# Sums of weight blocks on GpSimd, in two alternating buffers, in a two-layer hybrid decoder trunk

## The chip, the cores and the metric

The kernel runs on one core of one Trainium2 chip. The metric is the device time of one execution in microseconds (us). The time before is the median of three runs, 1335.95 us (1334.69 to 1336.82). Below, PE is the matrix engine (TensorE), PEld its weight loads, DVE VectorE, ACT ScalarE, POOL GpSimd, and SP the engine that issues the weight transfers.

## The reference, cut to what matters

Two layers over 528 positions (512 inputs behind 16 learned ones) of width 1024. Each layer is a token mixer and a gated feed-forward block with a causal convolution, each followed by a layer norm. The change touches the arithmetic of the projections only, so these lines matter:

```python
def short_conv_mixer(h, w_in, conv_w, w_out):
    b_gate, c_gate, xv = jnp.split(h @ w_in, 3, axis=-1)
    u = causal_dwconv(c_gate * xv, conv_w)
    return (b_gate * u) @ w_out

def conv_ffn(h, w_up, conv_w, w_down):
    u, gate = jnp.split(h @ w_up, 2, axis=-1)
    u = causal_dwconv(u, conv_w)
    return (jax.nn.silu(u) * gate) @ w_down
...
for i in range(DEPTH):
    ...   # mixer 0: chunked gated DeltaNet, mixer 1: short_conv_mixer
    h = layer_norm(ALPHA * h + mix, ln_mix_g[i], ln_mix_b[i])
    h = layer_norm(ALPHA * h + conv_ffn(h, ffn_w_up[i], ffn_conv[i], ffn_w_down[i]),
                   ln_ffn_g[i], ln_ffn_b[i])
```

## The kernel before

Activations lie channels down the partitions, positions along the row: `h` is 128 x 8 x 528 (8 blocks of 128 channels). Every float32 value that PE multiplies is split by `split` (L88, L89): ACT writes a rounded high part (`hh`, `gh`, `sumh`, and `wh` for weights), DVE the rest (`hl`, `gl`, `suml`, `wl`). A product is then three matmuls for each block of 128 rows, high by high, high by low, low by high (L272 to L274).

The order of stages is: the DeltaNet mixer (the first 370 us), its output projection, the first feed-forward block, the short convolution, the second feed-forward block. A feed-forward block works on its 22 channel strips in groups of 4, 6, 6 and 6 (`GROUPS`): an up stage makes the strips of `u` and `gate`, then `down` multiplies the group by its part of the down projection, eight output strips `pd` whose results DVE adds to `h` (L762 for the first group, L764 for later ones). The short convolution has groups of 2 and 6.

The first group of each block is computed plainly (`up`). The later groups go by **pairs** (`pairs`, L888): two weight strips and two halves of the positions form a 2 by 2 block product, which is computed with seven half-size products in place of eight, so the weights and the activations have to be added up in blocks first. A pair loads two raw strips, a and b. Its seven weight operands (`PREP`) are the blocks A11 and A12 (of a), A22 (of b) and four sums made by `sums`: S1 = both halves of b; S2 = S1 + A11; S3 = a half of b plus A11, written in place into b; S4 = S2 + A12. Before the change, DVE makes all four, and S1, S2 and S4 are one buffer `s`, overwritten in turn. There are 43 pairs in seven sections: three sections of 6 in each feed-forward block and one of 7 in the short convolution. On PE a pair takes its products in the order A11, S1, A22 of the pair before, S2, A12, S4 of the pair before, S3. A11, S2, S3 and A22 accumulate into one bank `px`, S1 and S4 into `pz`, and A12 goes to `pq`. Between the products ACT reads the running sum of `px` (L921 after A11, L927 after S2, L935 after S3, L940 after A22), and the next product into `px` cannot start before. DVE finishes with L932, L937, L944 and the gating (L846, L990). Six banks hold all of this.

The split weights live in a ring of 56 blocks (`room`): two tiles `wh0`/`wl0` and `wh1`/`wl1`. `pump` loads raw strips and splits them as far ahead as the ring and the raw buffers (four) allow. A scheduler fixes the order of each engine's instructions when the program is built, by its own timing model. On the chip each engine then takes its instructions strictly in that order, each waiting for its inputs.

The pools: `cpool` keeps constants for the whole run. `gp` holds the DeltaNet stage's buffers, and is given back when that stage ends; the later pools, `wpool2` with `s` among them, take that space.

Of the kernel before, what the change touches and what calls it, by code (L numbers as in the profile page):

```python
# [8 lines left out]
F32 = mybir.dt.float32  # L9
F32R = mybir.dt.float32r  # L10
F16 = mybir.dt.float16
U8 = mybir.dt.uint8
AF = mybir.ActivationFunctionType
ALU = mybir.AluOpType
PSUM = bass.MemoryType.PSUM

P = 128
# [13 lines left out]
CH = 106  # L31
# [3 lines left out]
LEVELS = (1, 2, 4, 8, 16, 32, 64)  # L35
# [18 lines left out]
NCST = 3 * P  # L54
# [19 lines left out]
def tile_hybrid_trunk(ctx, tc, xt, par, cst, msk, w_ba, w_qkv, w_z, w_ao, w_bi, w_bo, w_up, w_dn, out):  # L74
    nc = tc.nc
    V, S, G, TE = nc.vector, nc.scalar, nc.gpsimd, nc.tensor

    cpool = ctx.enter_context(tc.tile_pool(name="cpool", bufs=1))
    hpool = ctx.enter_context(tc.tile_pool(name="hpool", bufs=1))
    wpool = ctx.enter_context(tc.tile_pool(name="wpool", bufs=1))  # L80
    lnp = ctx.enter_context(tc.tile_pool(name="lnp", bufs=1))

    h = hpool.tile([P, KD, T], F32, name="h")
    hh = hpool.tile([P, KD, T], F32R, name="hh")
# [7 lines left out]


    par_sb = cpool.tile([P, NPAR], F32, name="par_sb")
    cst_sb = cpool.tile([P, NCST], F32, name="cst_sb")
    msk_sb = cpool.tile([P, len(LEVELS), CH], U8, name="msk_sb")
    ba_raw = lnp.tile([P, KD, 16], F32, name="ba_raw", tag="c", bufs=CB)
    ba_hi = lnp.tile([P, KD, 16], F32R, name="ba_hi", tag="c", bufs=CB)
    ba_lo = lnp.tile([P, KD, 16], F32R, name="ba_lo", tag="c", bufs=CB)
# [60 lines left out]
    pools = []  # L160
# [43 lines left out]
    def sums(job, what):  # L204

        a, b = job.raws
        a11, a12, a21, a22 = a[:, 0:4, :], a[:, 4:8, :], b[:, 0:4, :], b[:, 4:8, :]
        if what == "S1":
            job.s = pools[-1].tile([P, 4, P], F32, name=f"s{job.n}", tag="s", bufs=1)
            V.tensor_tensor(job.s, a21, a22, ALU.add)  # L210
        elif what == "S2":
            V.tensor_tensor(job.s, job.s, a11, ALU.add)
        elif what == "S3":
            V.tensor_tensor(a21, a21, a11, ALU.add)
        elif what == "S4":
            V.tensor_tensor(job.s, job.s, a12, ALU.add)
        own = {"A11": a11, "A12": a12, "A22": a22, "S3": a21}
        return own[what] if what in own else job.s

    def prep_step(job):  # L220

        pair = len(job.srcs) == 2
        what = PREP[len(job.units)] if pair else "all"
        u = room(4 if pair else job.nk)
        if u is None:
            return False
        job.units[what] = u
        if pair:
            split(u.hi, u.lo, sums(job, what))
        else:  # L230
            step = job.nk if job.n else 4
            for k in range(0, job.nk, step):
                split(u.hi[:, k : k + step, :], u.lo[:, k : k + step, :], job.raws[0][:, k : k + step, :])
        job.ready = len(job.units) == (len(PREP) if pair else 1)
        return True
# [50 lines left out]
    pump(2)  # L286

    ident = cst_sb[:, C_ID : C_ID + P]
    ident16 = cpool.tile([P, P], F16, name="ident16")
    V.tensor_copy(ident16, ident)  # L290
    tri = cst_sb[:CH, C_TRI : C_TRI + CH]
    strict = cst_sb[:CH, C_STR : C_STR + CH]
    strict_r = cpool.tile([P, CH], F32R, name="strict_r")
    V.tensor_copy(strict_r[:CH], strict)
    one1 = cpool.tile([P, P], F32, name="one1")
    V.memset(one1, 1.0)
    epsc = cpool.tile([P, 1], F32, name="epsc")
    V.memset(epsc, LN_EPS)
# [11 lines left out]
        return ap.unsqueeze(1).to_broadcast([ap.shape[0], n, ap.shape[1]])  # L310


    with ExitStack() as gctx:
        gp = gctx.enter_context(tc.tile_pool(name="gp", bufs=1))
        pm = gctx.enter_context(tc.tile_pool(name="pm", bufs=2, space=PSUM))
        pg = gctx.enter_context(tc.tile_pool(name="pg", bufs=2, space=PSUM))
        HB = T // 2
# [807 lines left out]
```

## Time and profile before

| | before |
|---|---|
| median of three runs | 1335.95 us |
| the profiled execution | 1335.62 us |
| its span, first to last instruction | 1333.8 us |
| PE busy | 1297.3 us, 97% |
| DVE busy | 1045.4 us, 78% |
| ACT busy | 780.8 us, 59% |
| POOL busy | 91.9 us, 7% |
| mean granted PE clock | 0.998 |

A row of a timeline gives start, duration, engine, line, operation, what is written and read, the shape and how many were merged; in brackets stands the idle time of the engine before it and what ended it. A row of groups gives the count, the busy time in us, the mean of one in ns, and the idle time before them. Buffer numbers are left out of names.

### The profile page before, as it was taken

The numbers are of one execution on the slowest core, as the hardware profiler recorded it, in microseconds if no ns is written. First come the engines' busy times: TensorE is split into PE (matmuls) and PEld (weight loads), VectorE is DVE, ScalarE is ACT, GpSimd is POOL, SyncE is SP. The second block draws the span as 40 slices with busy tenths as digits, with TensorE's granted clock in tenths as the row PEclk, the third lists the DMA queues.
The fourth block names the chain that finished last, engine by engine and source line by source line (L and its number), as shares of the span: only waits on it lengthen the run. The fifth ranks groups of instructions, "written<-read, shape, count | busy, mean of one in ns | idle before, by whom it ended". The sixth has DMA issues, their size and how long they took to land.

```text
span 1333.8 us, 26452 instructions
## 1 busy us (share of the span) xinstructions
PE 1297.3 (97%) x10687; PEld 1251.2 (94%) x10687; DVE 1045.4 (78%) x1909; ACT 780.8 (59%) x1629; POOL 91.9 (7%) x132
## 2 busy tenths in 40 slices
PE   7999999999999999999999999999999999999996
PEld 6899989999899999999999999999998998998996
DVE  6667676776467898969869789888789896986966
ACT  5676767776454846636537467455475563663744
POOL 0322332311110000000000000000000000000000
PEclk9999999999999999999999999999999999999999
DMA  5211111110161142522522422334024252242221
GB/s 200 64 49 33 49 48 34 48 49 33 48 218 59 35 150 66 157 64 87 151 64 81 142 70 62 107 95 158 18 80 127 96 144 78 83 139 73 81 70 64
DMA packets 38394, 115.85 MB, mean 87 GB/s; under 512 B 4224, under 2 KB 7808, under 8 KB 38272
## 3 DMA queue, kind: packets, MB, share of 16 engines
q1 hardware_dynamic: 37632, 112.04, 27.7%
q0 software_dynamic: 640, 2.12, 0.5%
q8 instruction: 83, 1.36, 0.4%
q14 instruction: 39, 0.32, 0.1%
HBM read 112.05 MB, written 2.10 MB: 86 GB/s over the span
## 4 chain that ended last, share of the span: by engine, by line
PE 81%; DVE 9%; ACT 5%; DMA 2%; issue 2%; POOL 2%; SPq 0%; ACTq 0%; POOLq 0%; DVEq 0%
PE pd L272 8%; PE pd L273 8%; PE pd L274 8%; PE px L272 6%; PE px L274 6%; PE px L273 6%; PE pz L272 3%; PE pz L273 3%; PE pz L274 3%; PE pu L273 2%; PE pu L274 2%; PE pu L272 2%; PE ps L274 2%; PE ps L273 2%; PE ps L272 2%
## 5 line engine op out<-in xcount | busy, mean ns | idle before, releaser
L88 ACT ACTIVATE wh<-raw 128x512 fp32r<-128x512 f32 (+3 forms) x319 | 237.7, 749 | 200.0 <-PE pd L273 82.1
L89 DVE TENSOR_TENSOR wl<-raw,wh 128x512 fp32r<-128x512 f32 (+3 forms) x319 | 264.9, 841 | 66.4 <-ACT wh L88 65.8
L272 PE MATMUL pd<-gh,wh 128*128 128x256 f32 (+3 forms) x704 | 213.6, 305 | 2.1 <-DVE h L762 1.3
L273 PE MATMUL pd<-gl,wh 128*128 128x256 f32 (+3 forms) x704 | 213.1, 303 | 0.0
L274 PE MATMUL pd<-gh,wl 128*128 128x256 f32 (+3 forms) x704 | 212.6, 302 | 0.0
L272 PEld LDWEIGHTS pd<-gh,wh 128*128 128x128 f32 x704 | 132.4, 189 | 8.4 <-DVE h L762 1.7
L273 PEld LDWEIGHTS pd<-gl,wh 128*128 128x128 f32 x704 | 132.8, 189 | 6.1 <-DVE gl L89 0.2
L274 PEld LDWEIGHTS pd<-gh,wl 128*128 128x128 f32 x704 | 132.8, 189 | 5.8
L88 ACT ACTIVATE wh<-s 128x512 fp32r<-128x512 f32 x129 | 81.3, 631 | 81.1 <-PE pd L273 34.5
L273 PE MATMUL pu<-hl,wh 128*128 128x258 f32 (+3 forms) x400 | 114.5, 289 | 1.5 <-DVE hl L743 1.4
L272 PE MATMUL ps<-hh,wh 128*128 128x264 f32 x384 | 114.5, 299 | 0.9 <-ACT acc L411 0.9
L274 PE MATMUL ps<-hh,wl 128*128 128x264 f32 x384 | 115.4, 301 | 0.0
L273 PE MATMUL ps<-hl,wh 128*128 128x264 f32 x384 | 114.3, 298 | 0.0
L274 PE MATMUL pu<-hh,wl 128*128 128x258 f32 (+3 forms) x400 | 113.4, 288 | 0.4 <-DVE wl L89 0.4
L272 PE MATMUL pu<-hh,wh 128*128 128x258 f32 (+3 forms) x400 | 113.4, 289 | 0.1
L89 DVE TENSOR_TENSOR wl<-s,wh 128x512 fp32r<-128x512 f32 x129 | 88.9, 689 | 13.9 <-ACT wh L88 11.2
L274 PE MATMUL px<-sumh,wl 128*128 128x258 f32 (+1 forms) x344 | 97.6, 284 | 0.0
L273 PE MATMUL px<-suml,wh 128*128 128x258 f32 (+1 forms) x344 | 97.4, 283 | 0.0
L272 PE MATMUL px<-sumh,wh 128*128 128x258 f32 (+1 forms) x344 | 97.4, 283 | 0.0
L272 PE MATMUL px<-hh,wh 128*128 128x258 f32 (+1 forms) x344 | 97.3, 283 | 0.0
L274 PE MATMUL px<-hh,wl 128*128 128x258 f32 (+1 forms) x344 | 97.0, 282 | 0.0
L273 PE MATMUL px<-hl,wh 128*128 128x258 f32 (+1 forms) x344 | 97.0, 282 | 0.0
(301 smaller groups left out, 3804.3 us busy)
## 6 DMA issues: line engine op xcount, KB each, us to landing
raw<-in_w_up_dram SPq DMA_DIRECT2D x88, 512.0 KB, 3.7
raw<-in_w_dn_dram SPq DMA_DIRECT2D x48, 384.0 KB, 3.4
raw<-in_w_bi_dram SPq DMA_DIRECT2D x24, 512.0 KB, 3.9
raw<-in_w_qkv_dram SPq DMA_DIRECT2D x23, 512.0 KB, 3.7
raw<-in_w_z_dram SPq DMA_DIRECT2D x8, 512.0 KB, 3.7
raw<-in_w_ao_dram SPq DMA_DIRECT2D x8, 512.0 KB, 3.7
raw<-in_w_dn_dram SPq DMA_DIRECT2D x16, 256.0 KB, 2.7
raw<-in_w_bo_dram SPq DMA_DIRECT2D x8, 384.0 KB, 3.5
```

What stands on the lines that cost most here:

```text
L88: S.activation(hi, src, AF.Copy)
L89: V.tensor_tensor(lo, src, hi.bitcast(F32), ALU.subtract)
L272: TE.matmul(ps, hi[:, k, :], r_h, start=start and k == 0, stop=False, **kw)
L273: TE.matmul(ps, hi[:, k, :], r_l, start=False, stop=False, **kw)
L274: TE.matmul(ps, lo[:, k, :], r_h, start=False, stop=stop and k == nk - 1, **kw)
```

## The change

The three lines that made S1, S2 and S4 in one buffer on DVE become one line that makes each in a fresh buffer on GpSimd; the tag `s` gets two buffers, so they alternate. S3 goes to GpSimd too, still in place. Five constants of the DeltaNet recurrence (`cst_sb`, `msk_sb`, `ident16`, `strict_r`, `one1`) move from `cpool` to `gp`, and `gp` is opened earlier, so that their space comes free with the rest of `gp`.

```diff
@@ -79,6 +79,8 @@
+    gctx = ExitStack()
+    gp = gctx.enter_context(tc.tile_pool(name="gp", bufs=1))
@@ -92,8 +94,8 @@
-    cst_sb = cpool.tile([P, NCST], F32, name="cst_sb")
-    msk_sb = cpool.tile([P, len(LEVELS), CH], U8, name="msk_sb")
+    cst_sb = gp.tile([P, NCST], F32, name="cst_sb")
+    msk_sb = gp.tile([P, len(LEVELS), CH], U8, name="msk_sb")
@@ -205,15 +207,12 @@
         a11, a12, a21, a22 = a[:, 0:4, :], a[:, 4:8, :], b[:, 0:4, :], b[:, 4:8, :]
-        if what == "S1":
-            job.s = pools[-1].tile([P, 4, P], F32, name=f"s{job.n}", tag="s", bufs=1)
-            V.tensor_tensor(job.s, a21, a22, ALU.add)
-        elif what == "S2":
-            V.tensor_tensor(job.s, job.s, a11, ALU.add)
+        if what in ("S1", "S2", "S4"):
+            old, other = (a21, a22) if what == "S1" else (job.s, a11 if what == "S2" else a12)
+            job.s = pools[-1].tile([P, 4, P], F32, name=f"{what}_{job.n}", tag="s", bufs=2)
+            G.tensor_tensor(job.s, old, other, ALU.add)
         elif what == "S3":
-            V.tensor_tensor(a21, a21, a11, ALU.add)
-        elif what == "S4":
-            V.tensor_tensor(job.s, job.s, a12, ALU.add)
+            G.tensor_tensor(a21, a21, a11, ALU.add)
@@ -286,13 +285,13 @@
-    ident16 = cpool.tile([P, P], F16, name="ident16")
+    ident16 = gp.tile([P, P], F16, name="ident16")
-    strict_r = cpool.tile([P, CH], F32R, name="strict_r")
+    strict_r = gp.tile([P, CH], F32R, name="strict_r")
-    one1 = cpool.tile([P, P], F32, name="one1")
+    one1 = gp.tile([P, P], F32, name="one1")
@@ -310,8 +309,7 @@
-    with ExitStack() as gctx:
-        gp = gctx.enter_context(tc.tile_pool(name="gp", bufs=1))
+    with gctx:
```

The lines below the changed ones stand two lower in the new kernel (L88 is L90, L762 is L760). Apart from numbers, the order of SP's transfers is the same in both programs, and so is PE's but for five matmuls. ACT and DVE keep their order outside the pairs. POOL, which had nothing to do after the DeltaNet stage, gets 172 additions.

The first place is the start of the first pair section, on ACT. Pair 56 is the first; its strips are `raw56` (a) and `raw57` (b), `c1_3` is the last gated strip of the plain group, and its high part `gh` is what PE waits for. Before:

```order
L88 ACTIVATE wh0_82<-raw57_6053 128x512
L88 ACTIVATE wh1_5015<-s56_6065 128x512
L88 ACTIVATE gh_5023<-c1_3_5964 128x516
L88 ACTIVATE wh0_82<-s56_6065 128x512
L88 ACTIVATE hh_68<-sc_5027 128x2x260
```

And now:

```order
L90 ACTIVATE wh0_85<-raw57_6053 128x512
L90 ACTIVATE wh1_5015<-S1_56_6065 128x512
L90 ACTIVATE gh_5023<-c1_3_5964 128x516
L90 ACTIVATE wh0_85<-S2_56_6123 128x512
L90 ACTIVATE wh0_85<-raw57_6053 128x512
L90 ACTIVATE wh0_85<-S4_56_6250 128x512
```

`gh` keeps its place behind the first sum, which is now POOL's. At this place PE's five matmuls of `pd1_1_1` that stood between the two groups of rows on the fourth strip stand behind them.

The second place is on DVE, in the short convolution, where its first `down` begins (`pd2_0_0` is the first of its result banks, freed by L762; `hl` is the low part of an activation block, `bu3` and `bc3` the convolution's strip). Before:

```order
L1019 TENSOR_TENSOR bc3_10479<-bc3_10479,pu108_9_0_10516 128x258
L89 TENSOR_TENSOR wl1_5016<-s116_10328,wh1_5015 128x512
L210 TENSOR_TENSOR s117_10578<-raw137_10324 128x512
L89 TENSOR_TENSOR hl_69<-sc_5027,hh_68 128x2x258 x2
L1019 TENSOR_TENSOR bc3_10479<-bc3_10479,pu108_9_1_10542 128x258
L89 TENSOR_TENSOR wl0_83<-s117_10578,wh0_82 128x512
L214 TENSOR_TENSOR raw137_10324<-raw137_10324,raw136_10322 128x512
L846 SCALAR_TENSOR_TENSOR bu3_10568<-bc3_10479,ntap_5028,bu3_10568 128x514
L212 TENSOR_TENSOR s117_10578<-s117_10578,raw136_10322 128x512
L846 SCALAR_TENSOR_TENSOR bu3_10568<-bc3_10479,ntap_5028,bu3_10568 128x514
L762 SCALAR_TENSOR_TENSOR h_67<-h_67,pd2_0_0_109_10585 128x258
```

And now:

```order
L1017 TENSOR_TENSOR bc3_10516<-bc3_10516,pu108_9_0_10554 128x258
L91 TENSOR_TENSOR hl_72<-sc_5027,hh_71 128x2x258
L91 TENSOR_TENSOR wl0_86<-S1_117_10616,wh0_85 128x512
L91 TENSOR_TENSOR hl_72<-sc_5027,hh_71 128x2x258
L1017 TENSOR_TENSOR bc3_10516<-bc3_10516,pu108_9_1_10580 128x258
L91 TENSOR_TENSOR wl0_86<-S2_117_10620,wh0_85 128x512
L760 SCALAR_TENSOR_TENSOR h_70<-h_70,pd2_0_0_109_10624 128x258
L844 SCALAR_TENSOR_TENSOR bu3_10606<-bc3_10516,ntap_5028,bu3_10606 128x514
```

The three sums are gone from the row; L760 now stands ahead of the convolution, and behind the low part of the second sum of pair 117.

The third place is ACT in the middle of a section, now (pair 73 runs on PE; its banks carry the number 74, those of pair 72 the number 73):

```order
L90 ACTIVATE wh1_5015<-S2_74_7896 128x512
L919 ACTIVATE sc_5027<-px74_7920 128x260
L90 ACTIVATE wh0_85<-raw86_7886 128x512
L90 ACTIVATE wh0_85<-S1_75_8021 128x512
L90 ACTIVATE wh0_85<-raw85_7759 128x512
L938 ACTIVATE pu73_7915<-px73_7791 128x260
L840 ACTIVATE c1_12_7960<-pu73_7915,ntap_5028 128x516
L925 ACTIVATE sc_5027<-px74_7920 128x260
```

Before, the conversion of S2 of pair 74 stood at the place where that of S1 of pair 75 stands now, and S1 of pair 74 where S2 of pair 74 does: the sums are converted earlier in relation to PE, by about a pair for S1.

## The prediction

> **What bounds the kernel now.** I read the page's busy times first, then windows over the pair sections, then all that PE waits for.
>
> ```profile
> PE 1297.3 (97%) x10687; PEld 1251.2 (94%) x10687; DVE 1045.4 (78%) x1909; ACT 780.8 (59%) x1629; POOL 91.9 (7%) x132
> ...
> core 0: us, PE busy (x) PEld busy (x) DVE busy (x) ACT busy (x) POOL busy (x), PEclk, DMA share, GB/s
> 600.00:700.00 100.00, 100.00 (x834) 99.75 (x833) 80.13 (x138) 51.97 (x96) 0.00 (x0) 1.00 0.34 100
> ...
> 610.70:620.80 10.10, 10.10 (x86) 10.10 (x85) 10.07 (x19) 7.05 (x14) 0.00 (x0) 1.00 0.25 64
> ```
>
> PE is busy in the whole of 600 to 700, pairs and `down` alike, at the full granted clock (1.00). The last window is one pair of the steady state: PE 10.10 us of 10.10, DVE 10.07. Both are full, but a busy PE could still be one that crawls, so I look at its starts.
>
> ```profile
> 620.68 0.28 PE L274 MATMUL px<-sumh,wl 128*128 128x260 f32 x1
> 620.80 0.28 PE L272 MATMUL px<-hh,wh 128*128 128x260 f32 x1
> ...
> PE pd L272 <- DVE h L762: 1.3, 1, 1.3
> ...
> PE pd L272 <- ACT gh L88: 0.7, 1, 0.7
> ```
>
> Matmuls start 0.12 us apart, and 84 of them (seven products of 12) make 84 x 0.12 = 10.1 us, the whole window. So nothing in a pair waits. The two rows of PE's waits are the only ones that lie where the sums are made: one before the first pair section, one in the short convolution. **PE sets the time, and a full DVE beside it costs nothing.**
>
> **How far the sums run ahead.** S1 of the pair that starts on PE at 620.80 was finished by DVE here:
>
> ```profile
> 611.34 0.69 DVE L210 TENSOR_TENSOR s<-raw 128x512 f32<-128x512 f32 x1
> 612.89 0.69 DVE L89 TENSOR_TENSOR wl<-s,wh 128x512 fp32r<-128x512 f32 x1
> ...
> 622.25 0.28 PE L272 MATMUL pz<-sumh,wh 128*128 128x260 f32 x1
> ```
>
> Its low part is written at 612.89 + 0.69 = 613.6, and PE first uses it at 622.25: 8.7 us spare. This is a sum made late in its section; the sections' first ones are made during `down`, with more.
>
> **What the change removes and adds.** DVE loses these 172 additions:
>
> ```profile
> L210 DVE TENSOR_TENSOR s<-raw 128x512 f32<-128x512 f32 x43 | 29.7, 690 | 1.3 <-DMA raw<-in_w_bi_dram 0.4
> L214 DVE TENSOR_TENSOR raw<-raw,raw 128x512 f32<-128x512 f32 x43 | 29.6, 688 | 0.4
> L212 DVE TENSOR_TENSOR s<-s,raw 128x512 f32<-128x512 f32 x43 | 29.6, 688 | 0.4
> L216 DVE TENSOR_TENSOR s<-s,raw 128x512 f32<-128x512 f32 x43 | 29.6, 688 | 0.2
> ```
>
> That is 118.5 us of DVE, 2.4 us of each pair (a row of two below takes 1.29 us, so they start 0.6 apart), all of it under a busy PE: worth nothing by itself. POOL's price for such an addition is not in the trace; its nearest row is a product of two float32 inputs:
>
> ```profile
> L479 POOL TENSOR_TENSOR NT<-NT,rk x8: 1072/1072/2602, 54.8 to 302.4; 106x530 f32<-106x530 f32 x8
> ```
>
> 1072 ns for 530 elements undisturbed gives 1.04 us for 512, and up to 2.6 when disturbed. Four of them are 4.2 us of a 10.1 us pair, so POOL is not full, and one sum is 0.35 us later than on DVE: hidden by the 8.7 us.
>
> **What disturbs whom.** The DeltaNet stage shows both engines together:
>
> ```profile
> 210.12 3.28 POOL L433 TENSOR_SCALAR bfE<-cst_sb,gA 106x106 f32<-106x106 f32 x1 [0.42 <-PE psE L437]
> ...
> 209.73 0.82 DVE L594 TENSOR_TENSOR oS<-oS,ro 106x640 f32<-106x640 f32 x1 [1.07 <-POOL ro L593]
> 210.47 0.77 DVE L415 SCALAR_TENSOR_TENSOR acc<-cb,par_sb,acc 128x528 f32<-128x528 f32 x1
> 211.15 1.22 DVE L89 TENSOR_TENSOR wl<-raw,wh 128x1024 fp32r<-128x1024 f32 x1
> 212.29 0.77 DVE L415 SCALAR_TENSOR_TENSOR acc<-cb,par_sb,acc 128x528 f32<-128x528 f32 x1
> ...
> 284.62 1.86 DVE L594 TENSOR_TENSOR oS<-oS,ro 106x640 f32<-106x640 f32 x1 [1.36 <-POOL ro L593]
> ...
> 284.55 1.24 POOL L396 TENSOR_TENSOR PT<-PT,cst_sb 106x530 f32<-106x530 f32 x1
> ```
>
> At 210 POOL's small instruction lasts until DVE's unbroken string of instructions with two inputs outside PSUM is over. At 284.6 the roles are exchanged: the 0.82 us instruction takes 1.86, starting in effect at 285.65, 0.14 before POOL's ends. So they exclude each other, and POOL holds DVE up for 1.04 - 0.14 = 0.9 us a sum. The rest of DVE's work in a pair:
>
> ```profile
> L846 DVE SCALAR_TENSOR_TENSOR c<-pu,ntap,c 128x516 f32<-128x516 f32 x5 | 3.8, 755 | 0.4 <-ACT c L842 0.3
> ...
> L944 DVE TENSOR_TENSOR pg<-sc,pz 128x260 f32<-128x260 f32 x2 | 0.9, 426 | 0.2 <-PE pz L274 0.2
> ```
>
> Taking off the 0.09 by which neighbours overlap, seven `wl`, `gl` and L990 at 0.6 and two L846 at 0.66 make 6.7 us; four sums 3.6; together 10.3. L944 and its like L932 and L937, which read PSUM, add 3 x 0.34 = 1.0 in which POOL may run. The two engines thus need between 10.3 and 11.3 us for a pair that PE does in 10.1, a lag of 0.2 to 1.2 a pair, where DVE alone just fitted. This lag is paid from the lead of 8.7 us and made up between sections, where DVE has room (80.1 of the 100 us from 600 to 700, a section and a `down`); while the last pair of a section runs, only plain strips are prepared. Cover and lag are near each other, and I cost it at nothing: the ends are 0, since PE has no wait in the pairs to lose, and the first rival's price.
>
> **The place before the first section.** PE waits for `gh`, which stands on ACT behind the first sum (shown in the order above).
>
> ```profile
> 477.41 0.28 PE L274 MATMUL pd<-gh,wl 128*128 128x260 f32 x1
> 478.42 0.74 PE L272 MATMUL pd<-gh,wh 128*128 128x260 f32 x4 [0.72 <-ACT gh L88]
> ...
> 475.28 1.29 DVE L89 TENSOR_TENSOR wl<-raw,wh 128x512 fp32r<-128x512 f32 x2
> 476.49 0.69 DVE L210 TENSOR_TENSOR s<-raw 128x512 f32<-128x512 f32 x1
> ...
> 478.64 0.69 DVE L89 TENSOR_TENSOR gl<-c,gh 128x516 fp32r<-128x516 f32 x1
> ...
> 476.32 0.63 ACT L88 ACTIVATE wh<-raw 128x512 fp32r<-128x512 f32 x1
> 477.21 0.63 ACT L88 ACTIVATE wh<-s 128x512 fp32r<-128x512 f32 x1 [0.26 <-DVE s L210]
> 477.75 0.62 ACT L88 ACTIVATE gh<-c 128x516 fp32r<-128x516 f32 x1
> ```
>
> POOL can start S1 when strip b has landed (by 476.32, when ACT converts it) and DVE's two `wl` let it, about 476.5: done 477.5, against 477.2. Then `wh` to 478.15, `gh` to 478.7: 0.35 late. `gl`, behind the sum's `wl` on DVE, comes at 479.45 or, if POOL's S2 gets in ahead, 480.4; before, five other matmuls (0.6 us) filled PE until then, and these now stand behind. Loss 0.35 to 1.6; I take 0.7, since the first of the two needs no lost race.
>
> **The place in the short convolution.** PE waits 1.5 us more than a step for a bank that L762 frees:
>
> ```profile
> 848.07 0.29 PE L274 MATMUL pd<-gh,wl 128*128 128x256 f32 x1
> 849.68 0.39 PE L272 MATMUL pd<-gh,wh 128*128 128x258 f32 x1 [1.33 <-DVE h L762]
> ...
> 836.26 0.69 DVE L210 TENSOR_TENSOR s<-raw 128x512 f32<-128x512 f32 x1 [0.41 <-DMA raw<-in_w_bi_dram]
> ...
> 849.21 0.42 DVE L762 SCALAR_TENSOR_TENSOR h<-h,pd 128x258 f32<-128x258 f32 x1
> ```
>
> From 836.3 on seven sums of 0.6 stand on DVE ahead of L762 (three of them in the order above), 4.2 us; without them the wait would be gone: -1.5. But L760 now stands behind S2 of pair 117, POOL's seventh sum from 836.3. Undisturbed that is 836.3 + 7 x 1.04 = 843.6, no wait. With turns taken as at 284, seven sums of 0.9, six turns of DVE of 0.6 between them, and three more instructions where DVE has two or three ready (as at 210), 836.3 + 6.3 + 3.6 + 1.8 + 0.14 = 848.1; then `wh` and `wl` at 0.65 each and L760's 0.42 end at 849.9, against 849.63: +0.3. Ends -1.5 and +1.0 (one more lost turn); I take +0.3, because the rows at 210 and 284 show such turns.
>
> **Constants and waits elsewhere.** The five constants change no instruction; up to the first pair ACT and DVE have the same order and PE and SP the same waits. A later pool may wait for `gp` to be given back, but `gp` already was before: 0, with ends of 0.1 either way.
>
> **The sum**, against the profiled execution's 1335.62 us (span 1333.8 and 1.8 around it, 0.33 below the median of the runs): +0.7 + 0.3 + 0 = **1336.6 us**. Its own range is the ends together: 1335.62 + 0.35 - 1.6 = 1334.4 to 1335.62 + 1.6 + 1.1 = 1338.3.
>
> **Rivals.**
>
> *The two engines become the bound, slower.* The point of decision is L927 (now L925), which ACT must finish before PE's S3.
>
> ```profile
> 616.76 0.37 ACT L927 ACTIVATE sc<-px 128x260 f32<-128x260 f32 x1
> ...
> 620.32 0.28 PE L274 MATMUL px<-sumh,wl 128*128 128x260 f32 x1
> ```
>
> The pair at 610.7 has S3 as its last 12 products, from 620.8 - 12 x 0.12 = 619.35, and L927 ends at 617.13: 2.2 us spare. Now it stands behind the conversion of S1 of a later pair, whose buffer comes free only after S2's `wl`. Sums taking turns with DVE use up that margin by 0.2 to 1.2 a pair; after two pairs PE waits by the lag. Leaving out two pairs and the last one of each section, 43 - 21 = 22 pairs pay the lower half of the lag, 0.2 to 0.7, as POOL gets in beside the PSUM readers: 4 to 15 us, 1340 to 1351, in the middle about 1346. For it: the rows at 210, and that 10.3 exceeds 10.1. Against: the lead, and gaps in DVE (80 us of 100 in a section with its `down`). Chance 0.28. The Trainium skill (SBUF — State Buffer, Who interferes with whom) has the mechanism as its rule: a VectorE instruction with two SBUF inputs and a GpSimd one that reads SBUF exclude each other, and the later one waits until the other has finished. By that rule the time would be this rival's 1346, against 1336.6 by the lead of the rows; the rows at 210 and 284 agree with it, and the one at 210 goes further, as POOL there waited out four instructions.
>
> *Both waits vanish, faster.* If sums and DVE hardly meet and POOL is early enough, 1.5 at 848 and 478.42 - 477.41 - 0.12 = 0.9 at 477 go: 1335.62 - 2.4 = 1333.2. Against: at 477 POOL cannot be ahead of DVE, as b lands only then. Chance 0.07.
>
> **How the numbers follow.** Forecast 0.65, slower rival 0.28, faster rival 0.07. A measurement of this kernel tells 0.2%, 2.7 us, from no change. The forecast's range lies inside that, so same 0.60, slower 0.33 (the rival, and 0.05 of the forecast's chance for more turns lost), faster 0.07. The range reaches from 1333.6, between the faster rival and the forecast's low end, to 1347, just past the slower rival's middle, which leaves out about half of either: some 2 in 10.
>
> **What would show it.** Right: POOL's additions at 1.0 to 2 us, PE 10.1 us a pair, waits of PE near 1.5 us at 477 and 848. Wrong towards slower: PE waiting for ACT's L925 inside pairs, and pair windows over 10.5 us. Wrong towards faster: no wait at 848, and `gh` at 477 not late. Sums near 1.04 throughout would refute the exclusion.

## The result, and the profile after

| kernel | median of its runs | ratio to before, 95% interval |
|---|---|---|
| before | 1336.38 us (4 runs) | |
| after | 1377.71 us (4 runs, 1376.45 to 1380.88) | 1.0316 (1.0304 to 1.0329) |

The change makes the kernel 41 us slower. The profiled execution of after took 1380.88 us (span 1379.1), against 1335.62 (span 1333.8) before, so the traces differ by 45.3 us; after's is the longest of its four. A matmul of 256 to 260 columns normally starts a step of 0.12 us after the one before. Adding up, over all matmuls after 465 us, how much later than its step each one starts (its lateness) gives 15.1 us before and 60.1 after; the difference, 45.0, is nearly the whole change of the span, and it lies in two kinds of place:

| lateness of matmuls, us | before | after |
|---|---|---|
| products of pairs (`px`, `pz`, `pq`) | 0.6 | 28.6 |
| `down` (`pd`), mostly ahead of a section, while its first sums are made | 4.6 | 21.9 |
| everything else | 9.9 | 9.7 |

What the conversions and the low parts of the sums took before, from the page of before:

```profile
L88 ACT ACTIVATE wh<-s 128x512 fp32r<-128x512 f32 x129 | 81.3, 631 | 81.1 <-PE pd L273 34.5
...
L89 DVE TENSOR_TENSOR wl<-s,wh 128x512 fp32r<-128x512 f32 x129 | 88.9, 689 | 13.9 <-ACT wh L88 11.2
```

From the page of after, engines and groups (count, then busy us and mean ns, then idle time before and what ended it), with the additions that were DVE's before:

```profile
PE 1314.8 (95%) x10687; PEld 1259.7 (91%) x10687; DVE 1060.2 (77%) x1737; ACT 776.6 (56%) x1629; POOL 344.1 (25%) x304
...
L213 POOL TENSOR_TENSOR S<-S,raw 128x512 f32<-128x512 f32 x86 | 124.4, 1447 | 258.3 <-DVE wl L91 252.5
L213 POOL TENSOR_TENSOR S<-raw 128x512 f32<-128x512 f32 x43 | 63.8, 1483 | 413.5 <-DMA raw<-in_w_up_dram 272.6
L90 ACT ACTIVATE wh<-S 128x512 fp32r<-128x512 f32 x129 | 81.2, 630 | 141.3 <-POOL S L213 79.9
...
L91 DVE TENSOR_TENSOR wl<-S,wh 128x512 fp32r<-128x512 f32 x129 | 111.0, 860 | 40.9 <-ACT wh L90 38.5
```

DVE lost 172 instructions (1909 to 1737) and is busy for *longer*, 1060.2 us against 1045.4: what stayed was stretched by more than the time that left with them. `wl<-S` takes 860 ns in the mean where it took 689. And ACT, in whose order the conversions of sums stand between other work, now waits 79.9 us for GpSimd's S1, S2 and S4, and 5.0 for S3. (Before, its waits for DVE's sums came to 50.6 us, in places where they cost PE nothing, so such a wait is not by itself a loss.)

What PE waits for (us in total, times, longest), from the waits of after:

```profile
PE px L271 <- ACT sc L925: 13.4, 15, 1.6
...
PE pd L272 <- DVE gl L91: 4.3, 3, 2.1
PE px L271 <- ACT sc L919: 3.4, 13, 0.3
PE pd L271 <- DVE bc L1017: 3.1, 2, 1.9
...
PE pd L271 <- ACT gh L90: 2.9, 2, 1.8
PE px L271 <- ACT sc L933: 1.4, 1, 1.4
```

None of the `px` rows was there before; most of the time is at L925. They add up to 18.2 us of idle time; lateness, from start to start, counts some 0.25 us more for each wait, and short delays that give no row.

**One of these waits, followed back.** Timeline of after in the fourth pair of the first section (pair 59; a row's last bracket is idle time before it, and its releaser):

```profile
535.03 2.98 POOL L213 TENSOR_TENSOR S<-S,raw 128x512 f32<-128x512 f32 x2 [5.36 <-DVE wl L91]
535.05 1.82 DVE L91 TENSOR_TENSOR gl<-c,gh 128x516 fp32r<-128x516 f32 x1
...
537.13 1.43 DVE L91 TENSOR_TENSOR wl<-raw,wh 128x512 fp32r<-128x512 f32 x1
...
538.49 0.68 DVE L91 TENSOR_TENSOR wl<-S,wh 128x512 fp32r<-128x512 f32 x1
...
539.30 1.61 POOL L213 TENSOR_TENSOR S<-raw 128x512 f32<-128x512 f32 x1 [1.29 <-issue]
540.95 0.63 ACT L90 ACTIVATE wh<-S 128x512 fp32r<-128x512 f32 x1 [3.17 <-POOL S L213]
...
541.61 0.28 PE L273 MATMUL pz<-hh,wl 128*128 128x260 f32 x1
...
543.03 0.37 ACT L925 ACTIVATE sc<-px 128x260 f32<-128x260 f32 x1
...
543.45 0.39 PE L271 MATMUL px<-sumh,wh 128*128 128x260 f32 x1 [1.57 <-ACT sc L925]
...
557.25 0.28 PE L271 MATMUL pz<-sumh,wh 128*128 128x260 f32 x1
```

Read it upwards from 543.45. PE wants S3's first product at 541.73, a step after 541.61, and starts it at 543.45, when L925 is done. L925 stood on ACT behind the conversion of S1_61 at 540.95 and three more instructions that fill ACT from there to 543.03, and ACT had been idle 3.17 us for that conversion. GpSimd made S1_61 from 539.30; the profile names no releaser ("issue"), but the buffer that S1_61 takes is that of S2_60, whose `wl` had ended at 539.17. That `wl` was late because GpSimd's two sums at 535.03 to 538.01 had stretched two DVE instructions ahead of it, from 0.69 to 1.82 and 1.43. And all this is for a sum whose product PE starts at 557.25 (last row), 14 us later. No sum came late to PE: of all 43 pairs the shortest time from the end of a sum's `wl` to its product is 8.3 us (7.2 before). What came late is the small evacuation behind it in ACT's order. This pair took 12.6 us in place of 10.1. In six of the seven sections the third, fourth and fifth pair take 0.6, 2.5 and 0.7 us more than before, and the second and the last nothing.

**A place ahead of a section**, at 477 us. GpSimd's rows are S2, S3 and S4 of the first pair; they and DVE's rows take strict turns:

```profile
478.52 1.60 POOL L213 TENSOR_TENSOR S<-S,raw 128x512 f32<-128x512 f32 x1
...
479.14 1.53 DVE L91 TENSOR_TENSOR wl<-S,wh 128x512 fp32r<-128x512 f32 x1
...
479.69 0.62 PE L271 MATMUL pd<-gh,wh 128*128 128x260 f32 x3 [1.81 <-ACT gh L90]
...
480.09 1.71 POOL L215 TENSOR_TENSOR raw<-raw,raw 128x512 f32<-128x512 f32 x1
...
480.60 1.75 DVE L91 TENSOR_TENSOR gl<-c,gh 128x516 fp32r<-128x516 f32 x1
...
481.76 1.73 POOL L213 TENSOR_TENSOR S<-S,raw 128x512 f32<-128x512 f32 x1
...
482.27 1.76 DVE L91 TENSOR_TENSOR wl<-S,wh 128x512 fp32r<-128x512 f32 x1
...
482.40 0.58 PE L272 MATMUL pd<-gl,wh 128*128 128x260 f32 x1 [2.10 <-DVE gl L91]
```

Undisturbed, GpSimd's instruction takes 1.28 us and DVE's 0.69; here every one of both engines takes 1.5 to 1.8, since it stands for a part of that time behind the other's. PE waits 1.81 us for `gh` and 2.10 for `gl`.

### The profile page after: what moved, and what is told of

Same layout as the page of the kernel before. It is cut to its first block, busy times and chain, and to the rows that moved or that the text cites. A ratio compares the mean times of both kernels' runs of the same rounds, so it can differ in the third digit from the quotient of the medians.

```text
span 1379.1 us, 26649 instructions
## 1 busy us (share of the span) xinstructions
PE 1314.8 (95%) x10687; PEld 1259.7 (91%) x10687; DVE 1060.2 (77%) x1737; ACT 776.6 (56%) x1629; POOL 344.1 (25%) x304
## 4 chain that ended last, share of the span: by engine, by line
PE 65%; DVE 17%; issue 6%; ACT 6%; POOL 4%; DMA 1%; SPq 0%; ACTq 0%; DVEq 0%; POOLq 0%
PE pd L272 8%; PE pd L271 8%; PE pd L273 8%; DVE wl L91 5%; PE px L271 3%; PE px L272 3%; PE px L273 3%; PE pu L273 3%; PE pu L272 3%; PE pu L271 3%; POOL S L213 2%; DVE c L844 2%; PE pz L271 2%; PE pz L272 2%; PE ps L273 2%
## 5 line engine op out<-in xcount | busy, mean ns | idle before, releaser
L91 DVE TENSOR_TENSOR wl<-raw,wh 128x512 fp32r<-128x512 f32 (+3 forms) x319 | 320.2, 1011 | 65.3 <-ACT wh L90 64.6
L90 ACT ACTIVATE wh<-raw 128x512 fp32r<-128x512 f32 (+3 forms) x319 | 236.7, 747 | 173.1 <-PE pd L272 94.6
L271 PE MATMUL pd<-gh,wh 128*128 128x256 f32 (+3 forms) x704 | 216.8, 309 | 6.6 <-DVE bc L1017 3.1
L272 PE MATMUL pd<-gl,wh 128*128 128x256 f32 (+3 forms) x704 | 216.6, 308 | 4.3 <-DVE gl L91 4.3
L273 PE MATMUL pd<-gh,wl 128*128 128x256 f32 (+3 forms) x704 | 215.8, 307 | 0.0
L213 POOL TENSOR_TENSOR S<-S,raw 128x512 f32<-128x512 f32 x86 | 124.4, 1447 | 258.3 <-DVE wl L91 252.5
L213 POOL TENSOR_TENSOR S<-raw 128x512 f32<-128x512 f32 x43 | 63.8, 1483 | 413.5 <-DMA raw<-in_w_up_dram 272.6
L90 ACT ACTIVATE wh<-S 128x512 fp32r<-128x512 f32 x129 | 81.2, 630 | 141.3 <-POOL S L213 79.9
L272 PEld LDWEIGHTS pd<-gl,wh 128*128 128x128 f32 x704 | 136.0, 193 | 11.1 <-DVE gl L91 5.2
L91 DVE TENSOR_TENSOR wl<-S,wh 128x512 fp32r<-128x512 f32 x129 | 111.0, 860 | 40.9 <-ACT wh L90 38.5
L273 PEld LDWEIGHTS pd<-gh,wl 128*128 128x128 f32 x704 | 136.0, 193 | 5.8
L271 PE MATMUL px<-sumh,wh 128*128 128x258 f32 (+1 forms) x344 | 100.1, 291 | 16.8 <-ACT sc L925 13.4
```

Of the source, the lines that this page charges most:

```text
L90: S.activation(hi, src, AF.Copy)
L91: V.tensor_tensor(lo, src, hi.bitcast(F32), ALU.subtract)
L213: G.tensor_tensor(job.s, old, other, ALU.add)
L271: TE.matmul(ps, hi[:, k, :], r_h, start=start and k == 0, stop=False, **kw)
L272: TE.matmul(ps, hi[:, k, :], r_l, start=False, stop=False, **kw)
L273: TE.matmul(ps, lo[:, k, :], r_h, start=False, stop=stop and k == nk - 1, **kw)
```

## The experiments

Two theories stood against each other. **Exclusion**: GpSimd's additions and DVE's instructions with two inputs outside PSUM shut each other out, and the lag reaches PE through ACT. **Buffers and order**: with a second buffer the conversion of S1 of the next pair stands ahead of L925, and it waits for the low part of S2; the engine matters little. Later a third, **lateness**: the sum takes longer on GpSimd, and whatever stands behind it waits. All times are medians beside runs of the kernel before on the same chip; "pairs" and "down" are the lateness of matmuls, as in the table above (before: 0.6 and 4.6).

| run | us | ratio (95%) | pairs | down |
|---|---|---|---|---|
| e1_dve_two | 1334.86 | 0.9991 (0.9981 to 1.0000) | 0.2 | 3.6 |
| e13_dve_again | 1334.80 | 0.9987 (0.9978 to 0.9996) | 0.2 | 3.9 |
| e2_pool_one | 1390.82 | 1.0412 (1.0390 to 1.0434) | 45.0 | 18.6 |
| e3_pool_4buf | 1380.89 | 1.0338 (1.0323 to 1.0354) | 22.8 | 28.2 |
| e4_memset | 1333.40 | 0.9978 (0.9968 to 0.9987) | 0.2 | 3.1 |
| e5_memset3 | 1334.13 | 0.9983 (0.9974 to 0.9993) | 0.4 | 2.9 |
| e6_decoy | 1356.98 | 1.0154 (1.0139 to 1.0169) | 17.9 | 9.1 |
| e7_one_input | 1350.27 | 1.0110 (1.0093 to 1.0127) | 13.0 | 6.1 |
| e8_s3only | 1338.08 | 1.0015 (1.0006 to 1.0025) | 1.2 | 9.7 |
| e9_late | 1362.20 | 1.0193 (1.0177 to 1.0209) | 28.7 | 3.1 |
| e10_first | 1348.11 | 1.0089 (1.0075 to 1.0102) | 0.4 | 16.3 |
| e12_s1s3 | 1355.47 | 1.0140 (1.0127 to 1.0154) | 9.0 | 15.5 |
| e14_late_held | 1356.20 | 1.0143 (1.0126 to 1.0160) | 20.1 | 6.8 |
| e15_held | 1344.61 | 1.0064 (1.0049 to 1.0079) | 6.9 | 6.8 |

**Engine or buffers.** The engine alone undone, the engine alone done, and more buffers:

```diff
--- after
+++ e1_dve_two
-            G.tensor_tensor(job.s, old, other, ALU.add)
+            V.tensor_tensor(job.s, old, other, ALU.add)
...
-            G.tensor_tensor(a21, a21, a11, ALU.add)
+            V.tensor_tensor(a21, a21, a11, ALU.add)
```

```diff
--- before
+++ e2_pool_one
-            V.tensor_tensor(job.s, a21, a22, ALU.add)
+            G.tensor_tensor(job.s, a21, a22, ALU.add)
...
-            V.tensor_tensor(job.s, job.s, a12, ALU.add)
+            G.tensor_tensor(job.s, job.s, a12, ALU.add)
```

with S2 and S3 in the same way, and

```diff
--- after
+++ e3_pool_4buf
-            job.s = pools[-1].tile([P, 4, P], F32, name=f"{what}_{job.n}", tag="s", bufs=2)
+            job.s = pools[-1].tile([P, 4, P], F32, name=f"{what}_{job.n}", tag="s", bufs=4)
```

> The change with its four sums given back to DVE; two buffers and the moved constants stay. Exclusion theory (GpSimd's sums and DVE's two-input instructions shut each other out, and that is the whole loss): back to the time before, 1334 to 1340 us, low parts wl at 0.69 us. Buffer theory (with a second buffer the conversion of S1 of the next pair stands on ACT ahead of L925, which PE needs for S3, and S1 waits for the low part of S2; the engine matters little): most of the 41 us stay, 1360 to 1378, with PE waiting for L925 in every section of pairs.

> The kernel before with only the engine of its four sums changed to GpSimd: one buffer, summed in place, constants where they were. Exclusion theory: the loss is there in full or larger, 1370 to 1390 us, sums of 1.3 to 1.8 us, wl up to 1.8 us. Buffer theory: most of it is gone, 1336 to 1350, since S1 of the next pair can no longer be placed ahead of the evacuations.

> The change with four buffers for the sums in place of two. Exclusion theory: the two engines still need more than a pair's 10.1 us, so 1365 to 1385 us. Buffer theory: POOL no longer waits for the low part of the sum two before it (253 us of waits in the changed kernel fall under 80), and the 28 us lost inside the sections go, 1336 to 1355 us.

The buffer theory falls three times. With DVE making the sums in two buffers, S1's conversion still stands ahead of L925 and nothing is lost, so the constants and the second buffer cost nothing. With GpSimd and one buffer the loss is larger, 55 us, just above the range expected; there PE waits most for L921, the reading after A11 (22.6 us). With four buffers GpSimd's wait for `wl` is nearly gone, and the loss is about that of two (1.034 against 1.032):

```profile
L213 POOL TENSOR_TENSOR S<-raw 128x512 f32<-128x512 f32 x43 | 64.2, 1492 | 624.5 <-DMA raw<-in_w_up_dram 452.6
...
L213 POOL TENSOR_TENSOR S<-S,raw 128x512 f32<-128x512 f32 x86 | 141.0, 1639 | 17.8 <-DVE wl L91 14.8
```

In these two rows of e3_pool_4buf's page 252.5 us of waiting for `wl` have become 14.8; the additions meet DVE more often instead (1639 ns in the mean, not 1447), and PE waits 12.6 us for L933 and 3.4 for L925, in place of 13.4 for L925. The buffer chain at 541 us decided *where* the lag came out, not whether.

**Held or late.** In these, GpSimd's time on a sum is made up of instructions that do or do not read SBUF. The first five leave the sums out, the last their second term. The edit is shown at the line of S1, S2 and S4; S3, on `a21`, is changed alike (`sd` is a scratch tile, `z` a constant one).

```diff
-            G.tensor_tensor(job.s, old, other, ALU.add)
+++ e4_memset
+            G.memset(job.s, 0.5)
+++ e5_memset3
+            for _ in range(3):
+                G.memset(job.s, 0.5)
+++ e6_decoy
+            G.memset(job.s, 0.5)
+            G.tensor_tensor(state["sd"], job.s, job.s, ALU.add)
+++ e15_held
+            G.tensor_tensor(job.s, z, z, ALU.add)
+++ e14_late_held
+            G.tensor_tensor(job.s, z, z, ALU.add)
+            G.memset(job.s, 0.5)
+++ e7_one_input
+            G.tensor_scalar(job.s, old, 1.0, None, ALU.mult)
```

> The change with each of the four sums replaced by a GpSimd memset of the same 128x512 tile: the sums are left out, the place in the order and the buffers stay. Exclusion theory (it takes an instruction that reads SBUF on GpSimd): DVE's wl back to 0.69 us and the time back to 1334 to 1342 us. If any GpSimd instruction that writes SBUF holds DVE up, wl stays above 0.8 us on the mean and the time at 1350 to 1378. Buffer theory: the order is what costs, so the time stays above 1355.

> As e4_memset, but three memsets in a row for each sum: GpSimd then takes 3 x 0.53 = 1.58 us a sum, as long as a disturbed addition of the changed kernel (1.61), and reads nothing from SBUF. The sums are left out. Exclusion theory (the loss is DVE held up by additions that read SBUF): wl at 0.69 us, 1332 to 1338 us. Latency theory (the sum simply comes later to ACT, which waits in order ahead of the evacuations): 1355 to 1378 us, with PE waiting for L925.

> Each sum is replaced by one memset (0.53 us, which ACT and DVE wait for) and behind it an addition of the memset tile to itself into a scratch tile that nobody waits for: the sums are left out. Exclusion theory: DVE is held up as in the change, wl at 0.82 us or more on the mean, and the time is 1355 to 1385 us although no sum is late by itself. Latency theory: no dependent waits for the addition, 1332 to 1342 us.

e4_memset and e5_memset3 lose nothing. From the groups of e5_memset3:

```profile
L214 POOL MEMSET S<- 128x512 f32 x387 | 202.6, 527 | 523.4 <-DVE wl L91 509.9 <-ACT gh L90 1.1
...
L91 DVE TENSOR_TENSOR wl<-S,wh 128x512 fp32r<-128x512 f32 x129 | 89.2, 691 | 46.0 <-ACT wh L90 43.6 <-PE pq L274 2.2
```

Three memsets keep GpSimd for 3 x 527 ns, as long as a disturbed sum of the change; `wl` stays at 691 ns and the time at 1334. **A sum that takes longer on GpSimd costs nothing by itself**, and neither does ACT's order. This holds for the time on GpSimd: a memset waits for no data, and ACT waits only 11.7 us for these, against 84.9 for the change's sums. Sums as late as those, but without a hold on DVE, were not tried. e4_memset also shows about what the change could have brought at best: sums for almost nothing are worth 0.22%. From the groups of e6_decoy:

```profile
L220 POOL TENSOR_TENSOR sd<-S 128x512 f32<-128x512 f32 x129 | 151.6, 1175 | 9.8
...
L91 DVE TENSOR_TENSOR wl<-S,wh 128x512 fp32r<-128x512 f32 x129 | 116.0, 902 | 20.6 <-ACT wh L90 20.4
```

Additions whose result nobody reads make `wl` 902 ns and the kernel 21 us slower. The next memset does stand behind them in GpSimd's order, but ACT waits for GpSimd even less than in e5_memset3, 7.8 us: **the hold on DVE costs, with hardly a late sum**. But 21 is half of 41. Two more kernels ask whether the rest is lateness on top of the hold.

> Each sum is replaced by an addition of a constant tile to itself, written where the sum goes, and behind it a memset of the same tile, for which ACT and DVE wait: 1.04 + 0.53 = 1.57 us a sum, late and with DVE held; the sums are left out. If lateness costs only together with the hold (both apart gave +22 for the hold and nothing for lateness, the change +41): 1368 to 1385 us. If the rest of the change's loss comes from its longer hold (an addition of two tiles takes 1.28 us, of one tile 1.04): 1353 to 1362 us as in e6_decoy.

> As e14_late_held without the memset: 1.04 us a sum undisturbed, DVE held; the sums are left out. If lateness and hold work together: between e6_decoy and e14_late_held, 1358 to 1372 us. If the hold alone sets the time: as e6_decoy, 1353 to 1361 us.

e15_held, at 1344.6, is faster than either expectation. With the same hold, half a microsecond more on each sum (e14_late_held against e15_held) costs 12 us, where longer sums cost nothing without a hold. But e14_late_held, with more GpSimd time on a sum than the change, is still 21 us short of it. Two things are left to differ. One is the length of the hold. An addition of a tile to itself takes 1.04 us undisturbed and makes a DVE instruction up to 0.9 us longer; one of two different tiles takes 1.28 and makes it up to 1.15 longer. In all, DVE's instructions after 470 us are 76 us longer than before in e14_late_held and e15_held, and 114 in after. The other is that in those two kernels a sum waits for no data: ACT waits 38.1 us for GpSimd in e14_late_held and 84.9 in after. Either may make the remaining 21 us, and I did not try the one without the other: this part stays open.

> Each GpSimd addition is replaced by a product of its first input with the constant 1, so that it reads one tensor of SBUF in place of two; the second term of the sums is left out, and every engine has the order of the change. If any GpSimd instruction that reads SBUF shuts DVE's two-input instructions out (as the Trainium skill, SBUF - State Buffer, Who interferes with whom, has it): wl above 0.8 us on the mean and 1350 to 1380 us. If two inputs on GpSimd are needed for it: wl at 0.69 us and 1333 to 1340 us.

The time lies at the lower end of the first range, but `wl`, at 733 ns, fits neither. The rows of e7_one_input's timeline at one place:

```profile
614.45 3.45 POOL L213 TENSOR_SCALAR S<-S 128x512 f32<-128x512 f32 x2 [8.81 <-DVE wl L91]
614.47 1.14 DVE L91 TENSOR_TENSOR gl<-c,gh 128x516 fp32r<-128x516 f32 x1
615.53 0.41 DVE L935 TENSOR_TENSOR pu<-sc,pz 128x260 f32<-128x260 f32 x1
615.87 0.68 DVE L91 TENSOR_TENSOR wl<-raw,wh 128x512 fp32r<-128x512 f32 x1
```

GpSimd's first product runs from 614.45 for 1.49 us; `gl`, which meets its start, takes 1.14 and not 0.69, but ends at 615.61, a third of a microsecond before it. So one input does hold DVE, by at most 0.47 us in this run, and not for the whole instruction. DVE's instructions are 23 us longer in all, and 14 us are lost, most of it in pairs, at L919 and L925. Why so little hold costs so much is not settled; that ACT waits for these sums nearly as long as for the change's is a likely part. Side by side, from the traces (the loss from the medians):

| run | DVE's instructions longer, us | ACT waits for GpSimd, us | lost, us |
|---|---|---|---|
| e5_memset3 | 1 | 11.7 | -2.0 |
| e6_decoy | 90 | 7.8 | 20.9 |
| e15_held | 76 | 18.3 | 9.0 |
| e14_late_held | 76 | 38.1 | 20.6 |
| e7_one_input | 23 | 70.5 | 14.2 |
| after | 114 | 84.9 | 41.3 |

Without a hold nothing is lost, but neither column alone gives the loss: e6_decoy loses 12 us more than e15_held with little more hold and fewer waits. Where the hold falls must count as well, and that is not resolved.

**Which sums, and how many.** `k` is the place of the pair in its section, from 0; both lines of `sums` that add go through `E` in the first two, and e8_s3only leaves the line of S3 on `G`.

```diff
+++ e9_late
+        E = G if k >= 2 else V
+++ e10_first
+        E = G if k < 2 else V
...
-            G.tensor_tensor(job.s, old, other, ALU.add)
+            E.tensor_tensor(job.s, old, other, ALU.add)
+++ e8_s3only
-            G.tensor_tensor(job.s, old, other, ALU.add)
+            V.tensor_tensor(job.s, old, other, ALU.add)
+++ e12_s1s3
-            G.tensor_tensor(job.s, old, other, ALU.add)
+            (G if what == "S1" else V).tensor_tensor(job.s, old, other, ALU.add)
```

> GpSimd makes the sums of the third and later pairs of each section alone (116 of 172); those of the first two pairs, which are made while `down` runs, are on DVE in the two buffers. By place: if the change's 45 us of PE's waiting are two separate losses, 28 inside the sections and 17 ahead of them, the 17 ahead go and the 28 stay: 1355 to 1365 us. If the losses hang together (DVE enters a section late, and pays for it there), less stays: 1340 to 1353 us.

> The other part: GpSimd makes the sums of the first two pairs of each section (56 of 172), the later ones are on DVE. Separate losses: the 17 us ahead of the sections stay and the 28 inside go, 1345 to 1355 us. If the loss comes from sums made during pairs alone: 1334 to 1339 us.

The loss inside the pairs is separate, almost to the number. What PE waits for in e9_late:

```profile
PE px L275 <- ACT sc L929: 13.5, 15, 1.6
...
PE px L275 <- ACT sc L923: 3.5, 13, 0.3
...
PE px L275 <- ACT sc L937: 1.4, 1, 1.4
```

and in e10_first:

```profile
PE pd L276 <- DVE gl L91: 2.5, 2, 2.1
PE pd L275 <- ACT gh L90: 2.2, 2, 1.1
PE pd L275 <- DVE h L764: 2.2, 1, 2.2
PE pd L275 <- DVE bc L1021: 1.9, 1, 1.9
```

The first are after's rows at L925, L919 and L933 (13.4, 3.4, 1.4) line for line, four lines further down; the second are the waits in `down`, and no product of a pair waits. 28.7 us are lost in pairs with the late sums alone, 28.6 with all. In `down` the first sums alone make 11.7 of the 17.3 us over before; the late ones alone make none, so a third of that loss needs both. It is mostly a wait at 574 us, which neither run has.

> Only S3, one of the four sums of a pair, on GpSimd; the other three on DVE in two buffers. Moved, a sum takes 0.6 us off DVE and holds it for some 1.15 us, so +0.55 us a pair against +2.2 us with all four. Lead theory (the lag is paid from the lead until it is used up): 6 x 0.55 = 3.3 us a section stays inside the lead of 8.7, 1333 to 1339 us. If the loss goes with the number of sums: a quarter of 41, some 1346 us.

> Two of the four sums, S1 and S3, on GpSimd. Lead theory: 6 x 2 x 0.55 = 6.6 us a section is still less than the lead of 8.7, so PE does not wait inside the sections and only the waits ahead of them grow, 1338 to 1346 us. If the loss goes with the number of sums: half of 41, some 1356 us.

One sum a pair costs almost nothing inside the sections (1.2 us), two cost 9.0, four 28.6: more than in proportion, as it would be if a reserve is used up first (which sums they are differs too). In `down` there seems to be no such reserve, as `gh` and `gl` are wanted at once: two sums cost 11 us there. One sum costs 5 in the trace of e8_s3only (9.7 against 4.6), but that is the longest of its ten executions, and 2.5 of it is a stretch at half speed (last section); by the medians e8_s3only loses 2.0 us in all, inside the lead theory's range. For e12_s1s3 that theory said under 1346 and no wait in pairs, and missed on both counts, 8 us in pairs and 11 in `down`. Its 1355 is what half of 41 gives, but the pairs alone are less than a third of theirs, so it is not a loss in proportion either.

> e1_dve_two once more with more rounds: whether two buffers and the moved constants, with the sums on DVE, beat the kernel before. The wait at 848 us was 0.68 in place of 1.62 there, so 0.5 to 1.2 us faster, a ratio of 0.9991 to 0.9996.

So two buffers with the sums on DVE are about 0.1% faster than the kernel before, a little more than expected, and this version beats both before and after: PE's pause at 848 us falls from 1.62 us to 0.84 between two starts.

## Why the prediction was wrong, step by step

- **The step that failed** is "Cover and lag are near each other, and I cost it at nothing". The lead of 8.7 us was there, and it still is (8.3 at the least); it was the wrong cover. The lag does not have to use up the lead of the sums, only the 2.2 us by which L925 is ahead of S3, since ACT works in order and holds L925 behind a sum that is wanted 14 us later. The signs that it had named for this came: waits for L925 inside pairs, and a pair of 12.6 us. The prediction named this point, with its mechanism and its margin, as the slower rival, and then gave it 0.28 because of the lead. That step was worth 28.0 us.
- **The price of a sum** was mis-sized: 1.04 us and a hold of 0.9, by the product `NT<-NT,rk`, whose second input is five columns repeated. The sums measured 1.28 undisturbed, and hold DVE up to 1.15. With these in the rival's own formula the two engines need 6.7 + 4 x 1.15 = 11.3 to 12.3 us a pair, a lag of 1.2 to 2.2, and 22 pairs at the lower half of it, 1.2 to 1.7, pay 26 to 37 us. The measured 28 lies there, and the rival's 4 to 15 came from the small hold. It fits as a mean: the pairs that pay are the ones the rival counted, but they pay 0.6, 2.5 and 0.7, not the same lag each. The Trainium skill (GPSIMD Engine Reference, Performance versus the Vector engine) has an addition of float32 on GpSimd at 1.96 times VectorE's time, at 2048 elements; by that an estimate would have been 1.96 x 0.69 = 1.35 us, nearer than the row I chose.
- **The place at 477** got +0.7 with an upper end of 1.6; it cost 5.9 (lateness from 1.2 to 7.1 us), 2.5 of it in a stretch at half speed (last section), which no term had. The order of events was as written, `gh` behind S1 and `gl` behind S2, but I let one turn be lost there. The rows above show turn after turn.
- **The place at 848** (869 now) got +0.3, with ends of -1.5 and +1.0; it cost 5.9 (7.7 us of lateness around that place against 1.8). Taking the sums from DVE did not remove the wait: e10_first still has 6.2 us of lateness there. The seven sums took 11.5 us, near the 11.8 that the prediction gave them, but PE waited for the two L1017, not for L760 (1.20 and 1.91 us), since each stands behind low parts stretched up to 1.77 us; 1.6 us more went in a stretch at half speed.
- **Places with no wait before** were left out of the sum. At 574 and 677 us PE waits for `gl` and `gh` now, 3.6 and 1.8 us. I had looked only where PE already waited; a new resource conflict makes its own places.
- **Constants and buffers at nothing** was right (e1_dve_two), and so was the exclusion itself, which the rows at 210 and 284 us had shown. The faster rival had its 2.4 us about right as a ceiling (2.3 in e4_memset), for sums that hold nothing.

## What to carry to other kernels

When an engine that is full gives work to one that it cannot run beside, count the pair of engines as one resource and add their times, at the price of the same operation on the same operands, before asking about cover. For cover, look at the smallest thing that stands behind the late work in an in-order queue, not at the slack of the late work itself. An upper bound first is cheap: replacing the moved work by nearly nothing showed that it was worth about 0.2% at best.

## What the runs showed of the hardware, unexpected

- **PE runs at half speed after some short stalls.** Windows of after (busy us and instructions of PE, PEld, DVE, ACT, POOL; granted clock; DMA share; GB/s):

```profile
574.30:576.50 2.20, 0.37 (x4) 0.16 (x2) 2.20 (x3) 0.00 (x0) 1.55 (x1) 1.00 0.25 101
...
577.00:580.40 3.40, 3.40 (x18) 3.40 (x17) 1.88 (x5) 0.63 (x1) 2.39 (x2) 0.51 0.00 0
580.40:590.00 9.60, 9.60 (x82) 9.60 (x81) 4.45 (x8) 2.53 (x4) 1.46 (x2) 1.00 0.36 109
...
873.70:880.70 7.00, 6.37 (x25) 5.49 (x26) 7.00 (x11) 1.87 (x3) 3.67 (x3) 0.52 0.00 1
```

  After a stall of 2.1 us at 574 (1.83 idle) and half a microsecond of full speed, matmuls start 0.215 us apart for 3.4 us, then 0.12 again. Besides one at its very end, the trace of after has three such stretches at a granted clock of 0.50, all in `down`: 6.83 us from 481.5, 3.41 from 577.1 and 6.83 from 874.0. At 0.095 us a matmul they are 5.5 of the 45 us, lost without any wait; the ten of e2_pool_one are 15 of its 59.

  Which stalls do it is a matter of place more than of length. In each trace the granted clock changes only on a grid of 3.413 us. Dividing the sixteen traces into its cells, 37 of the 39 at full speed in which PE idles 1.8 us or more are followed by half speed (both others lie at the very end of a kernel), and none with less than 1.6. The stall at 574 lies within one cell. That of 1.57 us idle at 541 is cut by the grid into 1.05 and 0.5, and one of 1.83 at 573.8 in e3_pool_4buf into 0.97 and 0.87: no stretch follows either. The Trainium skill (TensorE: Matmul & The Clock Gate, Part 1) has a free-running window of about 3.4 us behind the clock gate, and the grid agrees; it names an idle window as what lowers the clock, and here about half a window idle was enough.
- **A GpSimd product of one tile with a constant is slower than an addition of two tiles**, 1.49 us against 1.28 undisturbed, and holds DVE for less. The Trainium skill (SBUF — State Buffer, SBUF: two separate sides) has the holder keep the shared ports for the whole instruction; for the additions the runs nearly agree (1.15 of 1.28 us), for the product they don't (at most 0.47 of 1.49).
